# The first microseconds of a decoder layer: products of ones ahead of the operands, first weights through ACT's queue, the first product by blocks of D

## The chip, the cores and the metric

One Trainium2 chip, and of it one core. The metric is the time of one execution on the device in microseconds (us), the median of several runs. The engines are named as in the profile: PE (matrix products, with PEld for loading the stationary operand), DVE (elementwise vector work), ACT (activations, copies), POOL (more elementwise work), SP (issues DMA transfers). ACT can issue DMA transfers too, from a queue of its own.

## The reference

One layer (DEPTH is 1) of a hybrid decoder for 1024 prompt tokens and 64 sample tokens, D_MODEL 1024, D_FF 2816, all in float32:

```python
x = layer_norm(ALPHA * x + 0.5 * swiglu(x, f1_wg, f1_wu, f1_wd), ln1_g, ln1_b)   # first FFN
z = x @ w_in + b_in                                 # gMLP heads and mLSTM heads from one projection
...
mix = concatenate([head_rms(gm, gm_out_g), head_rms(h_ml, ml_out_g)])
x = layer_norm(ALPHA * x + mix @ w_out, ln2_g, ln2_b)
x = layer_norm(ALPHA * x + 0.5 * swiglu(x, f2_wg, f2_wu, f2_wd), ln3_g, ln3_b)   # second FFN

def swiglu(x, wg, wu, wd):
    return (jax.nn.silu(x @ wg) * (x @ wu)) @ wd
```

The change touches the products `x @ wg` and `x @ wu` of the two FFNs, which run the same code, and in the first FFN the loads that come before them.

## The kernel before, in words

The kernel is written in a tile framework. The Python code emits instructions in program order; the framework puts in the semaphores and fixes for each engine the order in which it takes them. It may move an instruction ahead of an earlier one of the same engine whose operands it expects later. On the chip each engine then takes its list strictly in that order, so one late operand holds everything behind it on that engine.

**Precision.** A float32 operand is split by `split` (L234 to L239) into a high part (an ACT cast to fp32r, L238, or L373 for weights) and the rest (a DVE subtraction, L239, or L374). A product of two split operands takes three matmuls, listed in `PROD`: high by high, high weight by low x, low weight by high x.

**The up product.** The two halves of D and the two halves of the prompt's tokens make x a matrix of 2 by 2 blocks; pairs of 128 hidden columns do the same for the weights. The class `Up` computes the four block products by seven products of sums and differences, numbered 1 to 7, for each of 11 pairs p of hidden columns. A step is (p, m): the product m of pair p, for gate (gu 0) and up (gu 1). Each of the two takes four blocks k of 128 rows of D by three matmuls, 128x512 each: 24 matmuls for a step (`product`, L376 to L384, which also calls `bg.tick()` after each k). `xo[m]` is the split x operand of product m, and `uop` the split weight operand. Product 1 needs the block of x with the first half of D and the first tokens (`xo[1]`, loaded as `rx["11"]` in four pieces of 128x512), product 2 the second half of D (`xo[2]`, from `rx["21"]`). Products 6, 5, 7, 3, 4 need sums over all four blocks, made by `x_operands` on DVE (L528, L529, L534, L538, and the splits at L239), and sums of weight blocks (L363 to L365, L367). For the first two pairs (NPRE = 2) products 1 and 2 come first, so that the work starts before all of x has arrived: the steps before are (0,1), (0,2), (1,1), (1,2), then (0,6), (0,5), (0,7), (0,3), (0,4), (1,6) and so on. After a step with m of 1, 2, 5 or 4 the 64 sample tokens follow in eight small matmuls (`sample`, L398, PSUM tile psm, operand xs).

Results: product 1 goes to a PSUM tile px (pool of four, tag z) that stays to step (p,4), and is copied out by ACT (L438); product 2 goes to pz (pool of four, tag s) and is added on DVE to that copy (L441). For gate ACT then takes the silu (L416), and for up DVE multiplies (L418).

**The order of loads.** `Up.load` issues weight transfers (512 KB a block, tile ur, six buffers); the very first one, (0,1), goes in two halves (L344), the others whole (L346), all from SP. The start of the first FFN is written out at L858 to L890: SP issues the first piece of `rx["11"]` (L858), the two halves of the first weights (L344), the three other pieces (L861), the sample tokens (L866), the four pieces of `rx["21"]` (L855), three weight blocks (L346), the remaining two blocks of x (`xraw`, L883), constants (L889), and then weights for product 6. The framework lets eight transfers be under way; a further one waits for an earlier one.

**The second FFN.** Its x comes from the layer norm (L288 to L307) on the chip: each tile of 128 tokens is normed on DVE, transposed by PE (tp, L252), and copied out. This work runs in `bg`, a list of generators that `tick()` moves on by one step each. When `up.step(0)` of the second FFN starts, the tiles of the second half of the prompt are still being transposed, a few transposes at each tick.

Of the kernel before, what the change touches and what calls it, by code (L numbers as in the profile page):

```python
# [16 lines left out]
P = 128  # L17
# [26 lines left out]
UP_ORDER = (1, 2, 6, 5, 7, 3, 4)  # L44
DOWN_ORDER = (1, 2, 6, 5, 3, 7, 4)
NPRE = 2
CHUNKS = ((0, 10), (1, 2, 3), (4, 5), (6, 7, 8, 9))
DORD = tuple(p for pairs in CHUNKS for p in pairs)
LAST = NPAIR - 1
PROD = ((0, 0), (0, 1), (1, 0))  # L50
# [134 lines left out]
def trunk_kernel(ctx: ExitStack, tc: tile.TileContext, a):  # L185
    nc = tc.nc
    V, S, G, TE = nc.vector, nc.scalar, nc.gpsimd, nc.tensor
# [20 lines left out]
    junk = spare.bitcast(BF16)  # L208
# [13 lines left out]
    def psum_z(name):  # L222
        return psz.tile([P, 512], F32, tag="z", name=name)

    def psum_s(name):
        return pss.tile([P, 512], F32, tag="s", name=name)

    def xa_tile(pool, name):
        return pool.tile([P, 4, 2, 512], F32R, tag="xa", name=name)
# [4 lines left out]
    def split(dst, k, src):  # L234

        ix = (slice(None),) * k
        hi = dst[ix + (0,)]
        S.copy(hi, src)  # L238
        V.tensor_sub(dst[ix + (1,)], src, hi.bitcast(F32))  # L239
# [79 lines left out]
    class Up:  # L319


        def __init__(self, ffn, u2, xo, xs):
            self.ffn, self.u2, self.xo, self.xs = ffn, u2, xo, xs
            self.ct = self.stg = None
            self.steps = [(p, m) for p in range(NPRE) for m in (1, 2)]
            self.steps += [(p, m) for p in range(NPRE) for m in UP_ORDER[2:]]
            self.steps += [(p, m) for p in range(NPRE, NPAIR) for m in UP_ORDER]
            self.prepared = self.loaded = 0
            self.complete = False
            self.ops, self.raw, self.s1 = {}, {}, {}  # L330
            self.x, self.w, self.c, self.smp = {}, {}, {}, {}

        def load(self, upto):
            while self.loaded < min(upto, len(self.steps)):
                p, m = self.steps[self.loaded]
                pre = p < NPRE
                need = {1: (0,), 2: (1,)}.get(m, ()) if pre else {1: (0, 1), 2: (2, 3)}.get(m, ())
                if pre and m == 6:
                    need = (2, 3, 0, 1)
                for blk in need:  # L340
                    r = self.u2.tile([P, 1024], F32, tag="raw", name=f"ur{p}_{blk}", bufs=6)
                    if self.loaded == 0:
                        for j in range(2):
                            nc.sync.dma_start(r[:, j * 512:(j + 1) * 512], a["wu"][self.ffn, p, blk, :, j * 512:(j + 1) * 512])  # L344
                    else:
                        nc.sync.dma_start(r, a["wu"][self.ffn, p, blk])  # L346
                    self.raw[(p, blk)] = r
                self.loaded += 1
# [7 lines left out]
        def _prepare(self, p, m):  # L356

            a11, a12, a21, a22 = (self.raw.get((p, blk)) for blk in range(4))
            eng = V if p < NPRE else G
            if m == 6:  # L360
# [14 lines left out]
                units.append(op)  # L375
            self.ops[(p, m)] = units  # L376

        def product(self, ps, units, gu, m, start):
            for k in range(4):
                c0 = (k % 2) * 256 + gu * P  # L380
                for j, (wi, xi) in enumerate(PROD):
                    TE.matmul(ps, lhsT=units[k // 2][:, wi, c0:c0 + P], rhs=self.xo[m][:, k, xi, :],  # L382
                              start=start and k == 0 and j == 0, stop=k == 3 and j == 2, skip_group_check=True)
                bg.tick()  # L384

        def sample(self, p, units, m):
# [20 lines left out]
        def step(self, i):  # L407
            p, m = self.steps[i]
            self.prepare(i + UP_AHEAD)
            units = self.ops.pop((p, m))  # L410
            c = self.c.setdefault(p, {})

            def hidden(name, gu, src):

                if gu == 0:
                    S.activation(c[name, 0], src, AF.Silu)  # L416
                else:
                    V.scalar_tensor_tensor(c[name, 0], src, 0.5, c[name, 0], op0=ALU.mult, op1=ALU.mult)  # L418
                    c.pop((name, 1), None)

            for gu in range(2):
                if m in (1, 6, 7, 4):
                    if m == 1:
                        self.x[p, gu] = psum_z("px")
                    ps = self.x[p, gu]
                    self.product(ps, units, gu, m, m == 1)
                elif m == 2:
                    ps = psum_s("pz")
                    self.product(ps, units, gu, m, True)
                else:  # L430
                    if m == 5:
                        self.w[p, gu] = (psum_s if p < NPRE else psum_z)("pw")
                    ps = self.w[p, gu]
                    self.product(ps, units, gu, m, m == 5)
                if m in (1, 6, 5):
                    name = {1: "11", 6: "12", 5: "22"}[m]
                    c[name, gu] = self.ctile(name)
                    S.copy(c[name, gu], ps)  # L438
                elif m in (2, 7, 3):
                    name = {2: "11", 7: "22", 3: "12"}[m]  # L440
                    V.tensor_add(c[name, gu], c[name, gu], ps)  # L441
                    hidden(name, gu, c[name, gu])
                else:
                    if gu == 0:
                        c["21", 0] = self.ctile("21")
                    hidden("21", gu, ps)
            self.sample(p, units, m)
            if m == 4:
                bg.spawn(("hs", self.ffn, p), self.out_sample(p))
                if p < LAST:  # L450
                    bg.spawn(("h", self.ffn, p), self.out(p))
                else:
                    self.complete = True
            bg.tick()
# [96 lines left out]
    def up_pools(ffn):  # L551

        u2 = tc.alloc_tile_pool(name=f"u2{ffn}", bufs=2, side="right")
        xsp = tc.alloc_tile_pool(name=f"xs{ffn}", bufs=1, side="right")
        rxp = tc.alloc_tile_pool(name=f"rx{ffn}", bufs=1, side="right")
        rx = {"s": rxp.tile([P, 8, TS], F32, tag="t1", name="xsr")}
        rx.update({n: rxp.tile([P, 4, 512], F32, tag="rx" + n, name="rx" + n) for n in ("11", "21")})
        xs = xsp.tile([P, 3, 4, 2 * TS], F32R, tag="xs", name="xs")
        return xsp, u2, rxp, rx, xs
# [25 lines left out]
    class Down:  # L585


        def __init__(self, ffn):
            self.ffn = ffn
            self.items = [(ci, m, pair) for ci, pairs in enumerate(CHUNKS) for m in DOWN_ORDER for pair in pairs]  # L590
            self.n = 0
# [19 lines left out]
        def early(self):  # L611
# [6 lines left out]
            hs = h1[:, 3].rearrange("p s c -> p (s c)")  # L618
            for j, pair in enumerate(CHUNKS[0]):
                self.hsl[pair] = hs[:, j * 384:(j + 1) * 384].rearrange("p (a c) -> p a c", a=3)  # L620
# [7 lines left out]
        def fetch(self, upto):  # L628
            while self.fetched < min(upto, len(self.items)):
                ci, m, pair = self.items[self.fetched]  # L630
                self.fetched += 1
                if pair == LAST:
                    continue
                if ci == len(CHUNKS) - 1 and m == 7:
                    if self.hopx is None:
                        self.hopx = xa_tile(xap, "hopx")
                    hop = self.hopx[:, pair - CHUNKS[-1][0]]
                else:
# [55 lines left out]
    def down(dn, residual, on_tile):  # L694
# [17 lines left out]
        done = [0]  # L712
        for ci, pairs in enumerate(CHUNKS):
            last = ci == len(CHUNKS) - 1
# [133 lines left out]
    xsp, u2, rxp, rx, xs = up_pools(0)  # L848
    xo = {m: xa_tile(xap if m in (1, 2, 6) else xbp, f"xo{m}") for m in (1, 2, 6, 5, 7, 3)}
    x_raw(rx)  # L850
    up = Up(0, u2, xo, xs)

    def x_load(name, i, n=1):
        for kk in range(0, 4, n):
            nc.sync.dma_start(rx[name][:, kk:kk + n],  # L855
                              a["xT"][i, :, kk * 512:(kk + n) * 512].rearrange("p (k t) -> p k t", k=n))

    nc.sync.dma_start(rx["11"][:, 0], a["xT"][0, :, 0:512])  # L858
    up.load(1)
    for kk in range(1, 4):  # L860
        nc.sync.dma_start(rx["11"][:, kk], a["xT"][0, :, kk * 512:(kk + 1) * 512])  # L861
    up.prepare(1)
    for kk in range(4):
        split(xo[1][:, kk], 1, rx["11"][:, kk])
    xsr = rx["s"]
    nc.sync.dma_start(xsr.rearrange("p k t -> p (k t)"), a["xsT"])  # L866
    x_load("21", 1)
# [151 lines left out]
    def gtile(name, shape=(NT, H)):  # L1019
        return mx.tile([P] + list(shape), F32, tag="g_" + name, name="g_" + name)  # L1020

    lf, av, mm, mp = gtile("lf"), gtile("av"), gtile("mm"), gtile("mp")
    fl, wi, wk, dec = gtile("fl"), gtile("wi"), gtile("wk"), gtile("dec")
# [545 lines left out]
    xsp, u2, rxp, rx, xs = up_pools(1)  # L1569
# [8 lines left out]
    up = Up(1, u2, xo, xs)  # L1578
# [159 lines left out]
```

## Time and profile before

| | |
|---|---|
| median of 3 runs | 1966.47 us (1965.08 to 1966.61) |
| profiled execution, whole time | 1967.1 us |
| its span, first to last instruction | 1965.3 us |
| mean granted TensorE clock | 0.995 |
| PE, DVE, ACT, POOL busy | 98%, 67%, 39%, 24% |
| PE idle before its first matmul | 6.05 us |
| first FFN, up products begin | 6.05 us |
| second FFN, up products begin | 1238.91 us |

A row of the timeline gives start, duration, engine, line, operation, output<-inputs, shape and count, and in brackets the idle time of the engine before it and what ended that. "PE" rows are matmuls, "PEld" rows the loads of the stationary operand; "SPq" rows are SP issuing transfers, not the transfers themselves. A row of the windows gives for a stretch of time its length, then the busy time of PE, PEld, DVE, ACT and POOL with counts, then the granted clock, the DMA engines' mean share and GB/s.

### The profile page before, as it was taken

What the parts mean: (1) busy time and instruction counts of PE and PEld (TensorE: products, weight loads), DVE (VectorE), ACT (ScalarE), POOL (GpSimd) and SP (SyncE); (2) the same over time, 40 slices, a digit from 0 to 9 for tenths busy, and PEclk for the clock granted to TensorE, in tenths of its full rate; (3) what the DMA queues carried; (4) which work ended last, traced back from release to release, by engine and by line L of the source; (5) the groups of instructions that cost most, each with busy time, mean ns of one, the idle gap of its engine ahead of it and who ended that gap; (6) DMA issues with size and microseconds to landing.
All of it is one profiled execution on the core that took longest, in us unless ns stands there. A gap on an engine that the chain in (4) does not pass through costs nothing.

```text
span 1965.3 us, 27416 instructions
## 1 busy us (share of the span) xinstructions
PE 1929.7 (98%) x10263; PEld 1637.7 (83%) x10263; DVE 1322.3 (67%) x2317; ACT 767.7 (39%) x1501; POOL 480.8 (24%) x404
## 2 busy tenths in 40 slices
PE   8999999999999999999999899999999999999997
PEld 6888888888788889988989899888888888878886
DVE  8866556656856585367776766986665655685657
ACT  5544444444212242164453333644444444422122
POOL 0222232222523031105423400112222222152302
PEclk9999999999999999999999999999999999999999
DMA  5444443337866532212111263244444433686643
GB/s 213 156 149 160 144 145 134 122 122 252 305 244 219 188 130 85 55 34 60 49 38 46 69 221 112 88 145 146 156 152 154 134 131 122 237 314 228 234 154 119
DMA packets 100893, 293.17 MB, mean 149 GB/s; under 512 B 19224, under 2 KB 26392, under 8 KB 97944
## 3 DMA queue, kind: packets, MB, share of 16 engines
q1 hardware_dynamic: 80600, 218.01, 33.7%
q10 hardware_dynamic: 20160, 73.41, 9.4%
q8 instruction: 81, 1.33, 0.3%
q14 instruction: 52, 0.43, 0.1%
HBM read 197.77 MB, written 93.60 MB: 148 GB/s over the span
## 4 chain that ended last, share of the span: by engine, by line
PE 51%; DVE 6%; POOL 2%; ACT 1%; issue 1%; DMA 1%; SPq 0%; DVEq 0%; ACTq 0%; POOLq 0%
PE px L382 12%; PE pw L382 6%; PE pd L737 5%; PE pw L737 4%; PE pw L944 4%; PE pq L964 4%; PE pz L382 3%; PE pv L944 3%; PE psm L398 2%; PE po L944 2%; PE pgm L944 1%; PE psm L746 1%; PE tp L252 1%; POOL grs L244 1%; DVE yb L307 1%
## 5 line engine op out<-in xcount | busy, mean ns | idle before, releaser
L382 PE MATMUL px<-xo,uop 128*128 128x512 f32 x2112 | 505.1, 394 | 6.3 <-ACT uop L373 6.2
L382 PEld LDWEIGHTS px<-xo,uop 128*128 128x128 f32 x2112 | 393.2, 189 | 91.6 <-ACT uop L373 6.4
L374 DVE TENSOR_TENSOR uop<-ur,uop 128x512 fp32r<-128x512 f32 x264 | 190.0, 736 | 113.9 <-ACT uop L373 113.6
L382 PE MATMUL pw<-xo,uop 128*128 128x512 f32 x1056 | 250.0, 392 | 0.0
L382 PEld LDWEIGHTS pw<-xo,uop 128*128 128x128 f32 x1056 | 198.1, 188 | 44.3
L737 PE MATMUL pd<-wop,hop 128*128 128x512 f32 x960 | 228.3, 394 | 4.4 <-ACT wop L238 2.6
L737 PEld LDWEIGHTS pd<-wop,hop 128*128 128x128 f32 x960 | 179.5, 188 | 48.2 <-ACT wop L238 3.4
L373 ACT CAST uop<-ur 128x512 fp32r<-128x512 f32 x264 | 158.8, 621 | 107.7 <-PE psm L398 72.9
L737 PE MATMUL pw<-wop,hop 128*128 128x512 f32 x792 | 188.5, 394 | 1.5 <-DVE hop L239 1.5
L737 PEld LDWEIGHTS pw<-wop,hop 128*128 128x128 f32 x792 | 147.9, 188 | 37.4 <-DVE hop L239 2.4
L238 ACT CAST wop<-wd 128x512 fp32r<-128x512 f32 x132 | 80.2, 621 | 246.9 <-DVE ya L708 120.0
L363 POOL TENSOR_TENSOR s<-ur,ur 128x1024 f32<-128x1024 f32 x18 | 43.3, 2404 | 510.6 <-DMA hd<-hw 262.3
L239 DVE TENSOR_TENSOR hw<-c,hw 128x512 fp32r<-128x512 f32 x120 | 96.5, 804 | 69.8 <-ACT hw L238 68.9
L382 PE MATMUL pz<-xo,uop 128*128 128x512 f32 x528 | 127.8, 397 | 0.0
L239 DVE TENSOR_TENSOR wop<-wd,wop 128x512 fp32r<-128x512 f32 x132 | 107.3, 824 | 27.3 <-ACT wop L238 26.8
L382 PEld LDWEIGHTS pz<-xo,uop 128*128 128x128 f32 x528 | 97.5, 188 | 22.4
L238 ACT CAST hw<-c 128x512 fp32r<-128x512 f32 x120 | 74.4, 620 | 73.5 <-DVE c L504 45.4
L944 PE MATMUL pgm<-w,xt 128*128 128x256 f32 x768 | 102.1, 289 | 0.9 <-ACT w L123 0.4
L398 PEld LDWEIGHTS psm<-uop,xs 128*128 128x128 f32 x704 | 95.3, 189 | 7.8 <-ACT uop L373 0.3
L944 PEld LDWEIGHTS pgm<-w,xt 128*128 128x128 f32 x768 | 95.4, 193 | 5.4 <-issue 3.5
L398 PE MATMUL psm<-uop,xs 128*128 128x256 f32 x704 | 97.9, 281 | 0.0
L944 PE MATMUL pw<-w,xt 128*128 128x256 f32 x768 | 97.3, 284 | 0.3 <-ACT xt L238 0.3
(334 smaller groups left out, 2885.2 us busy)
## 6 DMA issues: line engine op xcount, KB each, us to landing
hd<-hw ACTq DMA_DIRECT2D x140, 512.0 KB, 3.1
hop<-hd SPq DMA_DIRECT2D x132, 512.0 KB, 4.6
ur<-in_wu SPq DMA_DIRECT2D x94, 512.0 KB, 3.8
wd<-in_wd SPq DMA_DIRECT2D x22, 1024.0 KB, 8.3
wr<-in_ws SPq DMA_DIRECT2D x76, 256.0 KB, 2.8
hopx<-hd SPq DMA_DIRECT2D x8, 512.0 KB, 5.8
hsd<-sm SPq DMA_DIRECT2D x20, 192.0 KB, 2.2
hs<-hsd SPq DMA_DIRECT2D x18, 192.0 KB, 5.6
```

The source lines that it names most:

```text
L238: S.copy(hi, src)
L239: V.tensor_sub(dst[ix + (1,)], src, hi.bitcast(F32))
L244: G.tensor_tensor(out, t[:rows, :n], mh[:rows, :n], op=ALU.pow)
L252: TE.transpose(pv[:, j, :rows], y[:rows, t, c0:c0 + P], ident[:rows, :rows])
L363: eng.tensor_tensor(s1, a21, a22, op=ALU.add)
L373: S.copy(op[:, 0], sj)
L374: V.tensor_sub(op[:, 1], sj, op[:, 0].bitcast(F32))
L382: TE.matmul(ps, lhsT=units[k // 2][:, wi, c0:c0 + P], rhs=self.xo[m][:, k, xi, :], start=start and k == 0 and j == 0, stop=k == 3 and j == ...
L398: TE.matmul(ps, lhsT=self.xs[:, which, k, :], rhs=units[k // 2][:, wi, (k % 2) * 256:(k % 2 + 1) * 256], start=first and k == 0 and wi == ...
L737: TE.matmul(p, lhsT=hop[:, hi, i * P:(i + 1) * P], rhs=wop[:, wi, :], start=start and pi == 0 and j == 0, stop=pi == len(pairs) - 1 and j ...
L944: TE.matmul(p[:, :n], lhsT=xl(t, k, xi), rhs=wk[:, wi, kk * n:(kk + 1) * n], start=(i == 0), stop=(i == last - 1))
L964: TE.matmul(p[:, :n], lhsT=wk[:, wi, kk * P:(kk + 1) * P], rhs=rhs, start=(i == 0), stop=(i == (23 if c < 2 else 15)), skip_group_check=c ...
```

## The change

- Eleven matmuls (NWARM) of a 128x512 bf16 tile of ones, made by a DVE memset in the scratch tile `junk`, into a PSUM tile `warm` of tag s that nothing reads. They need no load.
- In the first FFN the two halves of the first weight block are issued by ACT instead of SP; in the second FFN the first block now comes whole, from SP.
- SP issues the four pieces of `rx["11"]` one after the other; the weights of the second step come before the sample tokens (`up.load(2)`).
- The steps of the first two pairs are reordered to (0,1), (1,1), (0,2), (1,2), in both FFNs.
- The first step of each FFN takes its matmuls by block k outside and gate/up inside, so that each block of D is used for both as it comes. In that step `bg.tick()` is no longer called between the blocks (it is still called once at its end).

```diff
+NWARM = 11
...
-            self.steps = [(p, m) for p in range(NPRE) for m in (1, 2)]
+            self.steps = [(p, m) for m in (1, 2) for p in range(NPRE)]
...
-                    if self.loaded == 0:
+                    if self.loaded == 0 and self.ffn == 0:
                         for j in range(2):
-                            nc.sync.dma_start(r[:, j * 512:(j + 1) * 512], ...)
+                            nc.scalar.dma_start(r[:, j * 512:(j + 1) * 512], ...)
...
+        def part(self, ps, units, gu, m, k, start):
+            c0 = (k % 2) * 256 + gu * P
+            for j, (wi, xi) in enumerate(PROD):
+                TE.matmul(ps, lhsT=units[k // 2][:, wi, c0:c0 + P], rhs=self.xo[m][:, k, xi, :],
+                          start=start and k == 0 and j == 0, stop=k == 3 and j == 2, skip_group_check=True)
+
         def product(self, ps, units, gu, m, start):
             for k in range(4):
...
+                self.part(ps, units, gu, m, k, start)
                 bg.tick()
...
-                    if m == 1:
+                    if m == 1 and (p, gu) not in self.x:
                         self.x[p, gu] = psum_z("px")
                     ps = self.x[p, gu]
-                    self.product(ps, units, gu, m, m == 1)
+                    if i > 0:
+                        self.product(ps, units, gu, m, m == 1)
+                    elif gu == 0:
+                        self.x[p, 1] = psum_z("px")
+                        for k in range(4):
+                            for g in range(2):
+                                self.part(self.x[p, g], units, g, m, k, True)
...
-    nc.sync.dma_start(rx["11"][:, 0], a["xT"][0, :, 0:512])
     up.load(1)
-    for kk in range(1, 4):
-        nc.sync.dma_start(rx["11"][:, kk], a["xT"][0, :, kk * 512:(kk + 1) * 512])
+    V.memset(junk[:, 0:512], 1.0)
+    warm = psum_s("warm")
+    for _ in range(NWARM):
+        TE.matmul(warm, lhsT=junk[:, 0:P], rhs=junk[:, 0:512], start=True, stop=True)
+    x_load("11", 0)
     up.prepare(1)
     for kk in range(4):
         split(xo[1][:, kk], 1, rx["11"][:, kk])
+    up.load(2)
```

More of the change, by code (lines that the diff above doesn't have):

```diff
@@ L341, in load @@
                     r = self.u2.tile([P, 1024], F32, tag="raw", name=f"ur{p}_{blk}", bufs=6)
-                    if self.loaded == 0:
+                    if self.loaded == 0 and self.ffn == 0:
                         for j in range(2):
-                            nc.sync.dma_start(r[:, j * 512:(j + 1) * 512], a["wu"][self.ffn, p, blk, :, j * 512:(j + 1) * 512])
+                            nc.scalar.dma_start(r[:, j * 512:(j + 1) * 512], a["wu"][self.ffn, p, blk, :, j * 512:(j + 1) * 512])
                     else:
@@ L376, in _prepare @@
             self.ops[(p, m)] = units
+        def part(self, ps, units, gu, m, k, start):
[3 more added lines that the diff above has]
+                          start=start and k == 0 and j == 0, stop=k == 3 and j == 2, skip_group_check=True)
         def product(self, ps, units, gu, m, start):
             for k in range(4):
[L380 to L383, printed above, removed]
+                self.part(ps, units, gu, m, k, start)
                 bg.tick()
```

## The prediction, made before the changed kernel ran

> **What bounds the kernel now.** I read the page first, then the timeline of the first 20 us, then the groups by line for the length of one matmul, then DVE's timeline up to step (0,6), and last the start of the second FFN. The page says that PE is the bound of the whole:
>
> ```profile
> span 1965.3 us, 27416 instructions
> PE 1929.7 (98%) x10263; PEld 1637.7 (83%) x10263; DVE 1322.3 (67%) x2317; ACT 767.7 (39%) x1501; POOL 480.8 (24%) x404
> ```
>
> So 35.6 us of the span have no matmul, and the change can reach those before the first one and a few behind it. The start in the timeline:
>
> ```profile
> 0.73 0.39 SPq L858 DMA_DIRECT2D rx<-in_xT  x1
> 1.17 0.90 SPq L344 DMA_DIRECT2D ur<-in_wu  x2
> 2.11 1.38 SPq L861 DMA_DIRECT2D rx<-in_xT  x3
> ...
> 4.72 0.62 ACT L238 CAST xo<-rx 128x512 fp32r<-128x512 f32 x1 [2.72 <-DMA rx<-in_xT]
> 5.37 0.69 DVE L239 TENSOR_TENSOR xo<-rx,xo 128x512 fp32r<-128x512 f32 x1 [5.37 <-ACT xo L238]
> ...
> 6.05 8.98 PE L382 MATMUL px<-xo,uop 128*128 128x512 f32 x24 [6.05 <-ACT uop L373]
> ...
> 9.33 0.62 ACT L238 CAST xo<-rx 128x512 fp32r<-128x512 f32 x1 [0.85 <-DMA rx<-in_xT]
> 9.98 0.69 DVE L239 TENSOR_TENSOR xo<-rx,xo 128x512 fp32r<-128x512 f32 x1 [0.78 <-ACT xo L238]
> 10.00 2.35 SPq L883 DMA_DIRECT2D xraw<-in_xT  x4
> 10.01 0.71 ACT L238 CAST xs<-xsr 128x256 fp32r<-128x256 f32 x2
> ...
> 14.88 1.10 PE L398 MATMUL psm<-uop,xs 128*128 128x256 f32 x8
> ```
>
> The first step runs from 6.05 to 14.88, 8.83 us. Two things stretch it. The fourth piece of x is waited for (9.33) and its low part is ready at 9.98 + 0.69 = 10.67; until then gate has three blocks, and the 12 matmuls of up follow after gate's. And the matmuls are long. These are two answers of the groups by line, of 9.2 to 9.8 us and of 12.8 to 13.4 us:
>
> ```profile
> L382 PE MATMUL px<-xo,uop 128*128 128x512 f32 x3 | 1.5, 628 | 0.0
> ...
> L382 PE MATMUL px<-xo,uop 128*128 128x512 f32 x4 | 1.1, 396 | 0.0
> ```
>
> The same matmul takes 628 ns and then 396 ns: until about 12.5 us PE is on a slow clock (the granted clock in the windows shows 1.00 there, so it is the durations that tell). From there on it is fast.
>
> Behind this step PE is not the only tight engine. DVE up to step (0,6), whose first matmul is the row at 35.71 (the next step is the last row):
>
> ```profile
> 16.21 2.50 DVE L374 TENSOR_TENSOR uop<-ur,uop 128x512 fp32r<-128x512 f32 x4 [0.30 <-ACT uop L373]
> 18.80 0.69 DVE L441 TENSOR_TENSOR c<-c,pz 128x512 f32<-128x512 f32 x1
> 19.41 1.22 DVE L528 TENSOR_TENSOR t<-xraw,rx 128x1024 f32<-128x1024 f32 x1
> 21.60 0.69 DVE L441 TENSOR_TENSOR c<-c,pz 128x512 f32<-128x512 f32 x1 [0.97 <-PE pz L382]
> 22.20 1.22 DVE L529 TENSOR_TENSOR rx<-xraw,t 128x1024 f32<-128x1024 f32 x1
> ...
> 35.29 1.22 DVE L534 TENSOR_TENSOR xraw<-xraw 128x1024 f32<-128x1024 f32 x1
> ...
> 35.71 1.20 PE L382 MATMUL px<-xo,uop 128*128 128x512 f32 x4 [0.18 <-ACT uop L373]
> 36.43 1.29 DVE L374 TENSOR_TENSOR uop<-ur,uop 128x512 fp32r<-128x512 f32 x2
> ...
> 41.89 5.68 PE L382 MATMUL pw<-xo,uop 128*128 128x512 f32 x24
> ```
>
> ```profile
> 0.00:14.60 14.60, 8.55 (x23) 6.03 (x24) 7.91 (x14) 9.48 (x17) 0.39 (x7) 1.00 0.84 288
> 14.60:35.70 21.10, 20.93 (x106) 17.44 (x105) 19.72 (x22) 12.81 (x18) 0.00 (x0) 1.00 0.64 251
> 35.70:60.00 24.30, 24.25 (x108) 19.70 (x109) 24.26 (x30) 12.88 (x21) 0.00 (x0) 1.00 0.28 88
> ```
>
> The last three rows are windows; DVE's busy time is the third pair. From 14.6 to 60 us DVE is busy for 43.98 of 45.40 us, and PE already waits for a weight operand at 35.71. A PE that comes earlier there finds nothing to do, unless DVE comes earlier too.
>
> **The change part by part.**
>
> *Products of ones.* Added: one memset and 11 matmuls. DVE is idle until 5.37, so the memset is hidden whatever it costs (the body starts at 0.73; a 128x512 DVE operation, 0.69 us, is its upper end). No row has a bf16 matmul of this size. Its spacing lies between that of the fast 128x512 matmul, (1274.39 - 1268.86) / 24 = 0.23 us by rows quoted below, and the slow duration, 0.63. I take 0.63 less the overlap of a fast one (0.39 - 0.23), 0.47, as nearest: 5.2 us for eleven, from about 1.2 (0.73 and most of a memset) to 6.4; by the ends eleven take 2.5 or 6.9, to 3.7 or 8.1. Up to 0.35 us of this may stand ahead of the first operands, ready at 6.05, and is covered by the wait for the fourth piece of x. Gain: before, 6.4 us passed from the first matmul to the fast clock; from 1.2 the same 6.4 us end at 7.6.
>
> *First weights by ACT.* Two issues (0.90 for both, as SP's) ahead of ACT's first cast at 4.72, when ACT had been idle for 2.72: hidden. SP is relieved of the same 0.90, so pieces 2 to 4 are issued at 1.17 instead of 2.11. They need not land earlier: the DMA engines are near full (a share of 0.84 over the first 14.6 us is 12.3 us, of some 13 after the first issue), and of six transfers of 256 KB the fourth piece is still the last. Ends: 0 and 0.94 earlier. I take 0, since the engines, not SP, are full.
>
> *Second weights ahead of the sample tokens.* 512 KB come between piece 4 and xsr. At 251 / 0.64 = 392 GB/s (the windows' rate by their share) that is 1.3 us: xsr, cast at 10.01 before, comes at 11.3 and its low part about 12.3, just when PE has finished step (0,1). Ends: a wait of 0.5 us, or none when step (1,1) is put ahead of those eight matmuls. I take none. Behind xsr everything on SP's list keeps its place, as one weight block less comes after `rx["21"]`.
>
> *Blocks of D outside.* When the last low part of x is there (10.67), six matmuls remain less one: 6 x 0.23 = 1.4, so step (0,1) ends at 12.1 instead of 14.88. PE gains 2.8 us there. Its ends: 1.4 (the six at the slow 0.47 take 2.8, to 13.5) and 3.7 with the fourth piece 0.94 earlier.
>
> *Step order.* Steps (1,1) and (0,2) change places; PE, ACT and DVE do the same work. What moves is DVE's: the adds of step (0,2) (L441, 18.80 and 21.60) now come one step later. Before, DVE sat idle for 0.97 at 21.60 because the add stood in its list ahead of ready work. Moved past: (0,2)'s weights come later than (1,1)'s, which are there before PE asks.
>
> *Then step (0,6).* PE would arrive 2.8 us earlier than 35.53 (35.71 less its 0.18). But its operand uop is split at 36.43 by DVE, after 17.7 us since 18.71 (the end of the four splits at 16.21) in which DVE was idle for 0.97 and 0.09 only. The work in between is the same after: thirteen operations spaced 1.14 (as 35.29 to 36.43), for xo[6], xo[5], the weight sums and L534, and three adds of 0.6 (18.80 to 19.41). What DVE can gain is those 1.06, plus what it starts earlier: 0.3 us, the wait for ACT in brackets at 16.21. So uop comes 1.4 us earlier, PE waits the rest, and everything behind (0,6) moves by 1.4. Upper end: if the scheduler puts those splits ahead of the L534 and xo[5] work that isn't needed yet (2.3 us directly ahead of 36.43), PE keeps its 2.8, and 0.7 of the 0.83 that step (0,6) now loses (41.89 - 35.53 = 6.36 instead of 5.53): 3.5. Lower end: DVE is held by a transfer or a badly placed add as now: 0.
>
> *Second FFN.* Here nothing is waited for from memory, but `product`'s eight ticks of step (0,1) go. Rows of its start, PE and DVE:
>
> ```profile
> 1238.91 0.94 PE L382 MATMUL px<-xo,uop 128*128 128x512 f32 x3
> ...
> 1245.05 1.06 PE L252 MATMUL tp<-cc,yb 128*128 128x128 f32 x8 [0.62 <-DVE yb L307]
> ...
> 1246.01 0.42 DVE L239 TENSOR_TENSOR xs<-xsr,xs 128x256 fp32r<-128x256 f32 x1
> ...
> 1248.60 1.19 PE L398 MATMUL psm<-uop,xs 128*128 128x256 f32 x8
> ...
> 1267.24 1.22 DVE L239 TENSOR_TENSOR xo<-rx,xo 128x1024 fp32r<-128x1024 f32 x1
> 1268.86 5.68 PE L382 MATMUL px<-xo,uop 128*128 128x512 f32 x24
> 1274.39 5.67 PE L382 MATMUL pw<-xo,uop 128*128 128x512 f32 x24
> ```
>
> The transposes move from step (0,1) into (1,1). The 24 matmuls then run without a break, from 1238.91 to 1244.4, and the eight for the samples find their operand only at 1246.43: a wait of 2.0 us, unless (1,1) is put ahead. In return PE no longer waits in the middle (0.62 for L307). Whatever it gains it gives back at 1268.86, as the operand of (0,6) is ready at 1268.46, 0.4 before: at most 0.4 gained, at most 2.0 - 0.6 = 1.4 lost. I take 0.
>
> *Sum.* 1967.1 (profiled) - 1.4 = 1965.7. The median of the runs stands 0.63 below the profiled one: 1965.1.
>
> **The rivals.** A change of under 0.2%, 3.9 us, is about what a measurement of this kernel cannot tell from none.
>
> (1) *PE keeps its lead.* DVE's list is reordered and (0,6) doesn't wait: 3.5 us, 1963.0. For it: 2.3 us of work not yet needed stand ahead of the split. Against: the splits stand behind the weight sums, which wait for loads whose order has not changed. Chance 0.24.
>
> (2) *One closing of the clock fewer, or one more.* Rows of the middle of the kernel, three of the timeline and one of the windows (the last but two of its columns is the granted clock):
>
> ```profile
> 921.09 0.80 PE L1285 MATMUL p<-ya,wt 128*128 128x130 f32 x2 [2.35 <-DVE wt L1254]
> ...
> 921.97 5.45 PE L964 MATMUL pq<-xt,w 128*128 128x512 f32 x12
> ...
> 929.27 3.03 PE L964 MATMUL pq<-xt,w 128*128 128x512 f32 x12
> ```
>
> ```profile
> 922.00:926.00 4.00, 4.00 (x12) 3.13 (x12) 2.72 (x7) 3.66 (x8) 0.39 (x1) 0.50 0.02 4
> ```
>
> After an idle time of 2.35 us the clock is halved and the same 12 matmuls cost 2.4 us more. A small shift may make that one go: 1965.1 - 2.4 = 1962.7, or 1960.6 together with (1). Chance that one goes 0.15, half of it with (1) or another gain that puts it beyond 0.2%.
>
> (3) *Slower: the new wait in the second FFN.* PE waits 2.0 us at about 1244.4 for the sample operand and that closes the clock, as the 2.35 did: 1.4 + 2.4 - 1.4 gives + 2.4, 1968.9. It decides from an idle time of some 2 us; with 1 us nothing happens. For it: DVE is saturated there and L239 follows two norm operations. Against: the scheduler has (1,1)'s ready matmuls to put in between. Chance 0.10. The Trainium skill ("TensorE: Matmul & The Clock Gate", Why this matters for your kernels) asks only that no idle gap exceed about 3 us; by that rule this wait would not close the clock and the case would end at 1965.1 + 1.4 = 1966.5. The rows above show a closing after 2.35, so here the trace is stricter than the page.
>
> (4) *Nothing comes through.* Transfers set DVE's pace up to (0,6) and the 2.8 us are all waited away: 1966.5. Chance 0.11.
>
> **How the numbers follow.** The forecast (1.4 us, 1965.1) has 0.40, (1) 0.24, (2) 0.15, (3) 0.10, (4) 0.11. Range: from (2) with most of (1), 1961.2, to (3), 1968.9, leaves out about 0.15. Faster by over 0.2% (under 1962.5): the half of (2) and a tail of (1), 0.18. Slower by over 0.2% (over 1970.4): (3) with the start's gain lost too, 0.08. Between: 0.74. The likeliest case's own range is 1963.9 to 1966.5.
>
> **What would show it.** Each step in the profile after: eleven short rows of the tile warm from about 1.2 us; px matmuls near 392 ns from 8 us on; the eight psm or the next px at about 12 instead of 14.88; ACT's issues ahead of 4.72; a PE wait of 1 to 2 us for uop ahead of (0,6), with DVE full; then every later step 1.4 earlier, to 1238. A (0,6) that starts 3 us earlier without a wait makes (1) right; a wait for xs at 1244 with a clock of 0.50 makes (3) right. The prediction is wrong altogether if the emission order far behind the start changes, in the mixer above all, which no row of before can exclude.

## The result and the profile after

The changed kernel takes 1977.41 us (median of 6 runs, 1976.39 to 1978.66) against 1966.54 us before (also 6 runs): 10.9 us longer, a ratio of 1.0055 (95% interval 1.0043 to 1.0067). The forecast was 1965.1, with a range from 1961.2 to 1968.9. The page of the profiled execution after (1976.39 us, the fastest of the six):

```profile
span 1974.6 us, 27426 instructions
PE 1933.1 (98%) x10274; PEld 1638.2 (83%) x10274; DVE 1321.4 (67%) x2318; ACT 769.0 (39%) x1501; POOL 480.3 (24%) x404
```

The span is 9.3 us longer, and PE's busy time only 3.4. The rest is a hole near the start. The timeline after:

```profile
0.73 0.89 ACTq L345 DMA_DIRECT2D ur<-in_wu  x2
...
1.45 4.88 PE L874 MATMUL warm<-spare 128*128 128x512 bf16 x11 [1.45 <-DVE spare L871]
...
5.46 0.62 ACT L374 CAST uop<-ur 128x512 fp32r<-128x512 f32 x1 [2.53 <-DMA ur<-in_wu]
...
6.85 0.62 ACT L374 CAST uop<-ur 128x512 fp32r<-128x512 f32 x1 [0.77 <-DMA ur<-in_wu]
7.37 2.18 ACT L239 CAST xo<-rx 128x512 fp32r<-128x512 f32 x4
...
7.69 0.90 SPq L347 DMA_DIRECT2D ur<-in_wu  x2
8.04 6.21 PE L382 MATMUL px<-xo,uop 128*128 128x512 f32 x24 [1.72 <-ACT xo L239]
...
13.02 4.21 SPq L347 DMA_DIRECT2D ur<-in_wu  x4
...
14.09 1.11 PE L402 MATMUL psm<-uop,xs 128*128 128x256 f32 x8
15.03 5.72 PE L382 MATMUL px<-xo,uop 128*128 128x512 f32 x24
20.59 1.12 PE L402 MATMUL psm<-uop,xs 128*128 128x256 f32 x8
...
25.88 2.94 ACT L239 CAST xo<-xraw 128x1024 fp32r<-128x1024 f32 x3
28.73 2.18 ACT L374 CAST uop<-ur 128x512 fp32r<-128x512 f32 x4
29.39 1.22 PE L382 MATMUL pz<-xo,uop 128*128 128x512 f32 x2 [7.69 <-ACT uop L374]
31.05 6.71 PE L382 MATMUL pz<-xo,uop 128*128 128x512 f32 x22 [0.43 <-DVE uop L375]
...
45.06 3.20 PE L382 MATMUL px<-xo,uop 128*128 128x512 f32 x13
```

PE ends step (1,1) at 21.7 and then stands for 7.69 us: the weights of step (0,2) are cast by ACT only at 28.73. Step (0,6), the px at 45.06, began at 35.71 before: 9.35 later, as much as the two spans differ. The windows after (the last but two of the columns is the granted clock) show a second loss: the clock is halved from within the hole until 34 us, so that the first matmuls behind it run slow.

```profile
23.80:29.40 5.60, 0.01 (x1) 0.01 (x1) 5.60 (x6) 4.56 (x6) 0.00 (x0) 0.50 0.33 123
29.40:34.00 4.60, 4.17 (x9) 2.87 (x10) 4.60 (x7) 2.45 (x4) 0.00 (x0) 0.50 0.09 13
```

Why so late? SP issues the weights of (0,2) and (1,2) at 7.69. The order in which the built program's instructions stand on ACT, with buffer numbers, answers it. A line has the place in ACT's list, the line of kernel.py, and output<-input. First the changed kernel, then the one of the first experiment:

```
20 L239 CAST xo3_151<-xraw_152 128x2x512 x2
21 L374 CAST uop0_2_232<-ur0_1_230 128x512
22 L374 CAST uop0_2_235<-ur0_1_230 128x512
23 L374 CAST uop1_2_277<-ur1_1_196 128x512
...
13 L377 CAST uop0_2_232<-ur0_1_194 128x512
14 L377 CAST uop0_2_235<-ur0_1_194 128x512
```

uop0_2 is the operand of step (0,2), ur0_1 block 1 of pair 0. It should come from buffer 194, the load at 7.69. It comes from 230, the last of the four blocks 2, 3, 0, 1 that are loaded for step (0,6), issued from 13.02. The cause is two lines of `prepare` (the comments are added here) and the one dictionary of loaded blocks:

```python
self.load(self.prepared + (3 if self.prepared else 1))   # prepared == 2: loads up to step 4, (0,6)
self._prepare(*self.steps[self.prepared])                 # step 2 then reads self.raw[(0, 1)]
```

In the old order step 2 was (1,1) and step 3 (1,2), of pair 1, whose blocks no load had replaced. In the new order step 2 is (0,2), and just before it is prepared the load for (0,6) puts a new tile under (0, 1). The values are the same, so nothing is wrong with the output: the operand is only taken from a copy that comes far later, and the first copy is never used.

### The profile page after: what moved, and what is told of

Same layout as the page of the kernel before. It is cut to its first block, busy times and chain, and to the rows that moved or that the text cites. A ratio compares the mean times of both kernels' runs of the same rounds, so it can differ in the third digit from the quotient of the medians.

```text
span 1974.6 us, 27426 instructions
## 1 busy us (share of the span) xinstructions
PE 1933.1 (98%) x10274; PEld 1638.2 (83%) x10274; DVE 1321.4 (67%) x2318; ACT 769.0 (39%) x1501; POOL 480.3 (24%) x404
## 3 DMA queue, kind: packets, MB, share of 16 engines
q8 instruction: 81, 1.33, 0.3%
## 4 chain that ended last, share of the span: by engine, by line
PE 50%; DVE 6%; POOL 2%; issue 2%; ACT 1%; DMA 1%; SPq 0%; DVEq 0%; ACTq 0%; POOLq 0%
PE px L382 12%; PE pw L382 6%; PE pd L748 5%; PE pw L959 5%; PE pw L748 4%; PE pq L979 4%; PE pz L382 3%; PE pv L959 3%; PE psm L402 2%; PE po L959 2%; PE psm L757 1%; PE tp L253 1%; POOL grs L245 1%; DVE ya L1372 0%; DVE ge L990 0%
```

## The experiments

All are variants of the changed kernel unless said otherwise. "Kept" means this edit, which gives each of the first steps its own block:

```diff
                     self.raw[(p, blk)] = r
+                    if pre and m in (1, 2):
+                        self.kept[(p, m)] = r
...
+            src = self.kept.get((p, m), src)
```

| run | edit | median us (runs) | ratio to before, 95% | (0,6) starts, us |
|---|---|---|---|---|
| before | | 1966.54 (6) | | 35.71 |
| after | | 1977.41 (6) | 1.0055, 1.0043 to 1.0067 | 45.06 |
| e1 | kept | 1966.27 (11) | 0.9998, 0.9989 to 1.0007 | 36.09 |
| e2 | before, new order alone | 1977.31 (5) | 1.0052, 1.0040 to 1.0065 | 46.02 |
| e3 | old order | 1967.11 (11) | 1.0003, 0.9994 to 1.0012 | 36.99 |
| e4 | kept, no ones | 1966.66 (11) | 0.9998, 0.9989 to 1.0007 | 36.15 |
| e5 | block 1 loaded first of four | 1972.80 (5) | 1.0033, 1.0020 to 1.0046 | 42.63 |
| e6 | hole filled with ones | 1973.66 (4) | 1.0039, 1.0025 to 1.0053 | 44.48 |
| e7 | kept, first weights by SP | 1966.59 (11) | 1.0000, 0.9991 to 1.0008 | 34.70 |
| e8 | kept, 15 ones | 1964.33 (11) | 0.9992, 0.9983 to 1.0000 | 35.03 |
| e9 | e7 with 15 ones | 1967.29 (11) | 1.0002, 0.9993 to 1.0010 | 35.41 |
| e10 | e9, weight sums on POOL | 1975.23 (5) | 1.0045, 1.0031 to 1.0059 | 38.19 |
| e11 | e8, weight sums on POOL | 1972.00 (6) | 1.0029, 1.0017 to 1.0040 | 36.25 |

Each ratio is to executions of the kernel before that were taken beside that run (medians 1966.36 to 1966.54). The starts of (0,6) and all profiles are of one execution each.

**e1, kept.** Each step splits the block that was loaded for it.

> The changed kernel, but each of the four first weight blocks of the pairs 0 and 1 is kept by its own step, so that step (0,2) splits the block that was loaded for it and not the one reloaded for step (0,6). Theory of the taken block: the wait of 7.7 us before (0,2) goes, step (0,6) starts at 32.5 to 35.5 us, and the time is 1963 to 1966.5. Rival, the list alone (the other edits make the scheduler put the casts of (0,2) behind those of x): the wait stays, 1976 to 1978.

The timeline of e1, PE:

```profile
15.60 1.10 PE L405 MATMUL psm<-uop,xs 128*128 128x256 f32 x8
16.54 5.73 PE L385 MATMUL px<-xo,uop 128*128 128x512 f32 x24
22.11 1.10 PE L405 MATMUL psm<-uop,xs 128*128 128x256 f32 x8
23.05 5.74 PE L385 MATMUL pz<-xo,uop 128*128 128x512 f32 x24
...
36.09 5.73 PE L385 MATMUL px<-xo,uop 128*128 128x512 f32 x24
```

The pz matmuls of (0,2) follow without a wait, and 11.1 us are gone. The rest of the change is worth nothing that can be measured: 0.9998 of before. (0,6) starts a little later than expected.

**e2, the new order alone.** The kernel before with one line changed.

```diff
-            self.steps = [(p, m) for p in range(NPRE) for m in (1, 2)]
+            self.steps = [(p, m) for m in (1, 2) for p in range(NPRE)]
```

> The kernel before with the new order of steps and nothing else. Theory of the taken block: the order alone brings the wait; PE stands for 5 to 8 us before (0,2), step (0,6) starts near 45 us, 1974 to 1978. Rival, the list alone: the other edits are what hurts, so this one stays within 2 us of 1966.5.

```profile
20.96 1.12 PE L398 MATMUL psm<-uop,xs 128*128 128x256 f32 x8
29.76 1.22 PE L382 MATMUL pz<-xo,uop 128*128 128x512 f32 x2 [7.68 <-ACT uop L373]
```

The same wait (7.68) and the same loss from the order alone. With e1 and e3 this shows that the order of steps, through the block taken from the later load, is the cause, and that neither the ones, nor ACT's queue, nor the blocks of D are needed for it.

**e3, everything but the order.** The line of e2 in reverse.

> The changed kernel with the old order of steps. Theory of the taken block: no wait of over 1 us before 35 us, 1963.5 to 1967. Rival, the list alone: a wait of several us ahead of the third step, 1974 to 1978.

No wait behind the first product, 1967.11, just above the interval that was expected. Its profile also shows that the ones do not always do their work. It begins as the changed kernel does (ones from 1.45, a gap of 1.73 us, the first px at 8.05), but the matmuls stay slow: step (0,1) ends at 16.51 instead of 14.09. These are the groups by line of 10 to 12 us, the changed kernel first, then e3:

```profile
L382 PE MATMUL px<-xo,uop 128*128 128x512 f32 x11 | 2.7, 395 | 0.0
...
L382 PE MATMUL px<-xo,uop 128*128 128x512 f32 x6 | 2.8, 628 | 0.0
```

The clock's records in the traces begin with its opening: at 6.71 in the changed kernel, at 14.13 in e3.

**e4, without the ones.** NWARM and the memset taken out of e1.

> As the kernel with the kept blocks, without the eleven products of ones. Theory that the ones are worth the clock: matmuls near 630 ns until 13 to 15 us, step (0,1) ends 1.5 to 3 us later; the time is 0 to 1.5 us longer than with them, since DVE sets step (0,6). Rival: the ones carry the gain through to the end, 2 to 3.5 us longer without them.

0.4 us more than e1, inside both intervals, and step (0,1) ends at 15.66 against 15.60. So in the profiled execution of e1 the eleven ones bought nothing at all, not even at the first step, which neither theory had. The windows of e1 say why:

```profile
8.00:10.00 2.00, 1.91 (x7) 1.30 (x8) 2.00 (x5) 2.00 (x5) 0.00 (x0) 0.97 1.01 386
10.00:13.30 3.30, 3.30 (x10) 2.54 (x9) 3.30 (x7) 3.25 (x8) 0.00 (x0) 0.50 1.05 402
```

The clock was fast at 8 and half from about 9.9 to 13.3: between the last of the ones (6.32) and the first px (8.02) PE stood for 1.70 us, the only such gap ahead of the closing. In the changed kernel a gap of 1.72 at the same place did not close it.

**e5, the taken block loaded first.** The changed kernel, with the late block three places earlier in the queue.

```diff
-                    need = (2, 3, 0, 1)
+                    need = (1, 2, 3, 0)
```

> The changed kernel with one edit: for product 6 of a pair the four weight blocks are loaded in the order 1, 2, 3, 0 instead of 2, 3, 0, 1, so that the block which step (0,2) takes comes first of four and not last. Theory of the taken block: three blocks of 512 KB at about 400 GB/s are 3.9 us, so the casts of (0,2) come some 4 to 7 us earlier (with what stands ahead of them on ACT), the wait shrinks from 7.7 to 1 to 4 us, (0,6) starts at 37 to 41, and the time is 1969 to 1973. Rival: the wait comes from how many casts stand ahead and not from this load; the time stays at 1976 to 1978.

```profile
25.42 1.28 PE L382 MATMUL pz<-xo,uop 128*128 128x512 f32 x3 [2.13 <-ACT uop L374]
28.09 7.24 PE L382 MATMUL pz<-xo,uop 128*128 128x512 f32 x21 [1.39 <-DVE uop L375]
```

(0,2) starts 3.97 us earlier than in the changed kernel, as three blocks at 400 GB/s give, and 4.6 us come back. The load decides. (0,6), at 42.63, was expected earlier: DVE's split of the second half is a new wait (1.39), and the first step ended at 15.70 instead of 14.09.

**e6, the hole filled.** The changed kernel, with thirty products of ones between (1,1) and (0,2).

> The changed kernel with thirty products of ones put before step (0,2), which fill PE's wait there for some 7 us at the fast clock. Theory that the closed clock is a part of the loss: the half clock of 23.8 to 34.0 goes; of it 29.4 to 34.0 had matmuls, so 2.3 us come back, (0,6) starts at 42.5 to 43, 1974.5 to 1975.5. Rival: the wait alone is the loss, as DVE and ACT are late anyway: (0,6) at 44.5 to 45, 1977.

```profile
30.91 1.19 PE L382 MATMUL pz<-xo,uop 128*128 128x512 f32 x4 [1.21 <-ACT uop L374]
...
44.48 5.68 PE L382 MATMUL px<-xo,uop 128*128 128x512 f32 x24
```

Mixed. The steps run at the fast clock (from (0,2) to (1,2), 30.91 to 38.13, 7.2 us instead of 9.2), but (0,2) starts 1.5 us later, and (0,6) is only 0.6 earlier, as the rival had it. The median is 3.8 lower all the same, most of it gained far behind the start: the changed kernel's profile has a closing of the clock at 508 us (0.57 from 508 to 512) that this one has not. So the closed clock cost about 2 us in that step; what it cost in the end is not settled by this run.

**e7, the first weights back on SP.** Kept, with the loads in the old order and place.

> The kernel with the kept blocks, with the first weights back on SP in the old place behind the first piece of x. Theory that ACT's queue costs the start: the first px goes at 6.0 instead of 8.0, the ones end at 6.3, the clock stays open, and step (0,1) ends at 12 to 12.5 instead of 15.6. If DVE sets (0,6), that step starts 1 to 1.6 us earlier than the 36.09 of the kept kernel and the time is 1964.5 to 1965.5. Rival: PE keeps the lead, (0,6) at 32.5 to 33, 1962.5 to 1963.5. Second rival: nothing comes through, 1966 to 1967.

```profile
5.86 6.26 PE L385 MATMUL px<-xo,uop 128*128 128x512 f32 x24
12.36 1.23 PE L405 MATMUL psm<-uop,xs 128*128 128x256 f32 x8 [0.24 <-DVE xs L240]
...
34.70 1.20 PE L385 MATMUL px<-xo,uop 128*128 128x512 f32 x4 [1.65 <-ACT uop L377]
```

```profile
12.40:34.70 22.30, 20.66 (x104) 17.38 (x104) 21.72 (x27) 14.67 (x22) 0.00 (x0) 1.00 0.68 267
```

The new queue and order of the first loads, which this run takes back together, did cost the start: the first px is back at 5.86, against 8.02 in e1, and step (0,1) is done 3.2 us earlier (a part of that is the clock that closed in e1). Of this PE keeps 1.4 at (0,6), where it waits for 1.65, with DVE busy for 21.72 of 22.30 us. The profiled execution took 1964.76, but the median of the eleven is 1966.59 (1964.76 to 1970.43), as the second rival had it. The steps of its profile are 1.0 us ahead of before up to 900 us, and 2.2 at the second FFN (1236.68 against 1238.91): the clock closes near 921 us in both, but in the kernel before it stays half for longer. The windows of that kernel and of e7:

```profile
924.80:927.20 2.40, 2.40 (x7) 1.86 (x6) 2.40 (x9) 1.78 (x6) 1.41 (x1) 0.50 0.14 19
...
924.80:927.20 2.40, 2.27 (x18) 1.90 (x16) 2.40 (x8) 0.99 (x3) 1.17 (x1) 1.00 0.46 119
```

So over half of that lead came far behind the start. The profiled execution was the fastest of the eleven, and what the 1.0 us at the start is worth in the median stays open.

**e8, 15 ones.** NWARM 15 in e1.

> The kernel with the kept blocks and 15 products of ones instead of 11, which last to about 7.5 to 7.9 and leave no gap of 1.7 us before the first px at 8.0. Theory that the gap closed the clock again at 9.9: it stays open, step (0,1) ends at 13.8 to 14.2 instead of 15.6; (0,6) starts 0 to 1.5 us earlier, 1964.8 to 1966.3. Rival: the ones are too long and push the first px, or DVE sets (0,6): no change to 1966.3.

The windows of e8:

```profile
14.50:35.00 20.50, 20.50 (x105) 17.29 (x104) 20.47 (x25) 15.02 (x22) 0.00 (x0) 1.00 0.63 246
35.00:60.00 25.00, 25.00 (x115) 20.60 (x114) 24.96 (x31) 11.60 (x20) 0.00 (x0) 1.00 0.27 85
```

The clock stays open, step (0,1) ends at 14.54 instead of 15.60, and 1964.33 is the best time seen: 2.2 us under before, with an interval that ends at no change. In its profile 1.1 us of the lead stand behind the start, up to 900 us; at the second FFN it is 2.7 (1236.24 against 1238.91), as the closings near 921 and 1091 us are shorter than those of the kernel before. How much of the median the fifteen ones earned is therefore not shown. The gap is not gone, though (1.59 us from 6.95), since the ones speed up once the clock opens: fifteen took 5.50 us, and at 0.44 each they would have taken 6.6. PE and DVE are both without a break from 14.5 to 60.

**e9, 15 ones with SP's loads.**

> The kernel with the kept blocks, first weights by SP, and 15 ones instead of 11, which end at 7.0 to 7.9, past the arrival of the first operands. Theory that DVE sets (0,6): the first px goes 1 to 2 us later than 5.86, step (0,1) ends 0 to 1 us later than 12.36, and (0,6) starts at 34.7 as with 11 ones. If the median of the kernel with 11 ones (1966.59, its profile 1.8 below) was lifted by runs in which a gap closed the clock at the start, this one comes to 1964 to 1965.5; if by closings later on, it stays at 1966 to 1967.

The median stays at 1967.29, so closings at the start were not what lifted e7's. (0,6) came at 35.41 after the same 1.65 of waiting, where 34.7 was expected: PE had waited 0.81 for xs, and 0.24 in e7. The profile of e9 (1967.51) has the other thing that was named, a closing later on. At 500 us its clock is half, where e7's is not; the windows of e7 and of e9:

```profile
500.10:503.40 3.30, 3.30 (x16) 2.68 (x15) 3.30 (x6) 2.18 (x4) 0.42 (x1) 1.00 0.91 268
...
500.10:503.40 3.30, 3.30 (x9) 2.52 (x10) 2.17 (x5) 0.00 (x0) 2.29 (x2) 0.50 0.28 51
```

How many executions of e7 have such a closing is not on record.

**e10 and e11, weight sums on POOL.** In the first FFN the sums of the first two pairs leave DVE.

```diff
-            eng = V if p < NPRE else G
+            eng = V if p < NPRE and self.ffn == 1 else G
```

> As the kernel with kept blocks, SP loads and 15 ones, with the sums of weight blocks of the first two pairs of the first FFN on POOL instead of DVE (three of 1.14 us for each pair). Theory that DVE sets (0,6): DVE is rid of 3.4 us ahead of it, (0,6) starts at 33 to 33.7 without a wait of over 0.5 us, 1 to 1.7 us earlier than with DVE, 1962.5 to 1964.5. Rival, the loads or ACT's casts set it: (0,6) stays at 34.5 to 35 or comes later, as POOL's three sums take 7.2 us after the last block at 25.5; no gain, 1964.5 to 1967.

> The kernel with kept blocks, ACT loads and 15 ones, whose (0,6) starts at 35.03 with no wait, with the same sums on POOL. Theory: there PE is the last (it comes to (0,6) at 35.03 and finds all ready), so taking work from DVE gives nothing at (0,6), 1963.8 to 1964.8. Rival: DVE's full list is behind later waits too, 1 us or more is gained, 1962.5 to 1963.5.

Against e9 and e8 they lost 7.9 and 7.7 us: misses of the first theory, and worse than the rival. The edit moves a fourth operation with them (L370). The timeline of e10, POOL, DVE and PE:

```profile
32.76 2.69 POOL L368 TENSOR_TENSOR ur<-s,ur 128x1024 f32<-128x1024 f32 x1
35.53 3.22 POOL L370 TENSOR_TENSOR ur<-ur,ur 128x1024 f32<-128x1024 f32 x1
...
25.85 1.22 DVE L543 TENSOR_TENSOR rx<-xraw,t 128x1024 f32<-128x1024 f32 x1
26.98 1.28 DVE L455 TENSOR_TENSOR c<-c,pz 128x512 f32<-128x512 f32 x2
...
33.16 3.38 DVE L548 TENSOR_TENSOR xraw<-xraw 128x1024 f32<-128x1024 f32 x1
36.46 3.38 DVE L240 TENSOR_TENSOR xo<-t,xo 128x1024 fp32r<-128x1024 f32 x1
...
38.19 0.75 PE L385 MATMUL px<-xo,uop 128*128 128x512 f32 x2 [3.83 <-ACT uop L377]
41.63 7.17 PE L385 MATMUL px<-xo,uop 128*128 128x512 f32 x22 [2.69 <-DVE uop L378]
```

While POOL adds, DVE's operation of 1.22 us takes 3.38. DVE was not relieved but slowed, the three sums end at 35.45, and PE pays for it in step (0,6): it waits 3.83 and 2.69 us in e10, and 2.81 in e11. Step (0,5) starts 7.1 us later than in e9 (48.64) and 5.9 later than in e8 (46.45), which is most of the loss.

## Why the prediction was wrong

**The step that failed** is "Step order", in the sentence that (0,2)'s weights come later than (1,1)'s "which are there before PE asks". The claim before it, that behind xsr everything on SP's list keeps its place, held, but did not help: the block that was read stood further back on that list. I followed the transfer, issued at 7.69, and took it that the step reads what was issued for it. It reads whatever the dictionary holds when the step is prepared, here a block whose casts came at 28.73, so that PE stood for 7.69 us. e2 has the whole loss from this line alone, 10.8 us, and e1 removes it. No row of the profile before could show it; the code could. None of the rivals named it, though (3) had the right shape, a new wait that closes the clock.

**First weights by ACT, taken as hidden: also wrong.** The issues were hidden, as said. But ACT's list now has both casts of the weights ahead of x (5.46 and 6.85, each waiting for its half), and x follows at 7.37. The first px came at 8.04 instead of 6.05, and e7 against e1 prices the new queue and order together at 2.2 us of the first px.

**Products of ones: the price right, the worth not.** Eleven took 4.88 us (estimated 5.2), a spacing of 0.44. The clock opened at 6.7 in the changed kernel. The 6.4 us from the first matmul to the fast clock, taken over from before, were no constant: it took 5.3 us there, 5.0 in e1 and 12.7 in e3, and 4.4 in e4 without ones. Nor was it foreseen that the first px moved away behind them, and that such a gap can close the clock again (e1).

**Blocks of D outside: right where its conditions held.** With SP's loads (e7) step (0,1) gave way to its samples at 12.36 after a wait of 0.24; the working had 12.1 and a wait of up to 0.5.

**Step (0,6): right.** In e7 PE came there early and waited for 1.65 (foreseen 1 to 2) with DVE full, and (0,6) began 1.0 us earlier than before, where 1.4 was worked out. In the median nothing of it can be told from no change.

**Second FFN: right.** After, from its first px to (0,6):

```profile
1248.14 7.17 PE L382 MATMUL px<-xo,uop 128*128 128x512 f32 x30
1255.76 1.18 PE L402 MATMUL psm<-uop,xs 128*128 128x256 f32 x8 [0.45 <-issue]
...
1277.87 5.68 PE L382 MATMUL px<-xo,uop 128*128 128x512 f32 x24
```

The scheduler put six matmuls of (1,1) ahead of the samples (30 and not 24), so that 0.45 of the wait of 2.0 was left; 29.73 us to (0,6) against 29.95 before. Here (0,2) takes the reloaded block as well, but PE waits for no weights between these rows.

## What to carry to other kernels

When the order of steps changes, follow each operand by the buffer that it is read from, in the built program's list, and not by the transfer that was meant for it: a table that is filled ahead can hand out a later copy, right in value and late in time. An opening that is shortened gives only what the next tight engine lets through, here DVE, so look at its idle time before pricing the gain. Products of ones that are to open a clock should last until the first real one, as they did in e7; with a gap behind them the clock closed again in e1 and opened late in e3. And one profile shows one execution: a closing of the clock that comes and goes far behind the edit can be worth as much as the edit.

## What the runs showed of the hardware that was not expected

- The clock closes after shorter idle times than 2.35 us: in e1 after 1.70, and in the changed kernel at 508 us after three waits of 1.33, 0.98 and 0.77 within 6 us, while the changed kernel's 1.72 and e8's 1.59 at the place of e1's gap left it open. So the length of one gap alone does not decide; what does is not settled by these runs.
- The same opening can find the clock differently: after the same eleven ones and nearly the same gap it was open from 6.71 in the changed kernel, and from 14.13 in e3.
- DVE and POOL slow each other: a DVE operation of 1.22 us on 128x1024 took 3.38 beside POOL's sums (e10). The Trainium skill ("SBUF — State Buffer", SBUF: two separate sides) says that a DVE operation with two SBUF inputs and a GpSimd (POOL) operation that reads SBUF exclude each other on a shared pair of ports, the loser waiting for the whole instruction. These rows agree: both stretched DVE operations end 1.09 us after the POOL operation beside them (36.54 after 35.45, 39.84 after 38.75), and the two additions at 26.98, which read one operand from PSUM, are not stretched.
